# Moving the later adaLN modulation of a two-layer RWKV/mLSTM/retention trunk from DVE sums in the projection stage to column products on PE in the RWKV stage

## The chip, the cores and the metric

The kernel runs on one core of one Trainium2 chip. The core has a matrix engine (PE, with its weight loader PEld), three engines for elementwise work (DVE, ACT, POOL) and SP, whose queue issues every DMA of this kernel, one after the other. The metric is the device time of one execution in microseconds, as the median of several runs: 3966.14 us before, from three runs between 3945.2 and 3976.5.

## The reference, cut to what matters

The reference is one inference step of a two-layer trunk over 128 context tokens and 1024 noisy tokens, width 1024. Each layer modulates its normalised input and its output by a conditioning vector:

```python
mod = silu(c) @ w_mod[l] + b_mod[l]              # 1024 -> 3072: shift, scale, gate
h = rmsnorm(x, norm_g) * (1 + scale) + shift
u = h @ w_in                                     # one projection for four head groups
y = concat(mlstm(u_a), rglru(u_b), retention(u_c), rwkv(u_d)) @ w_out
x = x + gate * y
```

There are two conditioning vectors (context and sample), so a modulation is a product of a 1024 x 3072 matrix with two columns, once for each layer. It is small in arithmetic and large in weights: 12 MB for each layer.

## The kernel before, in words

All is float32, with tokens along the free dimension and 128 channels along the partitions. The modulation of a layer is cut into six blocks (l, j) of 512 outputs; a block reads eight weight tiles of 128 x 512 (256 KB each). Blocks (0, 0) to (0, 3), which give shift and scale of layer 0, are computed at the very start. The other eight, listed in `MODS`, are the later ones: (0, 4) and (0, 5) give the gate of layer 0, (1, 0) to (1, 5) all of layer 1.

A layer has two long stages.

**The projection stage** (`in_proj`) walks over a list of jobs. A job loads a tile of `w_in`, splits it into two halves `wring_h` and `wring_l` (ACT, POOL), and multiplies both with the halves `hh` and `hl` of the input on PE, 24 products for each output tile, into one of two PSUM tiles named `main`. DVE and ACT in turn copy the result out (`st`, L1306 and L1304), and a DMA stores it. The jobs of kind C have the weights stationary (`main<-hh,wring_h` in the rows), those of kind T the tokens (`main<-wring_h,hh`). The mLSTM, RG-LRU and retention branches run beside the jobs as soon as their inputs are there. In layer 0 alone, every fourth job starts one later modulation: for each of the eight weight tiles (`wmod`, two buffers) and each of the two columns, DVE multiplies the 128 x 512 tile by one number for each partition and adds it to `macc` (L52, L48). After three more jobs PE sums `macc` over the partitions by products with a column of ones (`main<-ones,macc`, eight products) in a `main` tile, and DVE adds the bias into `mod`.

**The RWKV stage** (`rw_all`) runs through nine units, in nine periods. In a period, a chain of 16 steps alternates between PE and DVE (`u<-ST,AR`, DVE `UV`; `u<-UV,BT`, DVE `ST`), and between two steps lies a gap. DVE meanwhile solves triangular blocks of the next unit (`tm`, `iN`), whose input and result pass through DRAM (`dU`, `dN`, `SC`). To keep PE at work in the gaps, `pull` takes products of two other projections: the projections of RWKV's own inputs (`late_proj`, weights `w_in`) and the output projection (`out_proj`, weights `w_out`). These products (`main<-yt,ow`, L1312), 648 in a layer, are called fills here. A fill's weights come in tiles of the tag `ow`, with six buffers (`OWB`), four fills to a tile.

In this stage the products on PE stand in the order of the program (`pe` chains each one to the one before it), so PE cannot pass a product that waits. Elsewhere, and on the other engines and SP, a scheduler sets the order when the kernel is built, by priorities (`level`, `HP1`, `HP2`) and by its own estimate of times. A float32 product of the program is two instructions on PE in the trace, each with its own weight load.

Of the kernel before, what the change touches and what calls it, by code (L numbers as in the profile page):

```python
# [30 lines left out]
class B:  # L31
# [130 lines left out]
    def rw_all(self, l):  # L162
# [83 lines left out]
        for n, (p, su) in enumerate(units):  # L246
# [6 lines left out]
            for gap in range(16):  # L253
                with self.level(3):
                    next(steps)
                self.pull(rate)
                if gap == 1 and finish is not None:
                    with self.level(1):
                        self.rw_gate(finish)
                        self.rw_final(l, finish)  # L260
                    self.finished += 1
                    finish = None
                if gap == 1 and n + 1 == N:
                    with self.level(1):
                        self.rw_gate(P[p])
                if gap >= 2:
                    next(tok, None)
                if gap == 4 and n + 2 < N:
                    block(n + 2)
                    pre = early(n + 2)  # L270
                if gap in (12, 14):
                    next(pre, None)
            weave(tok, 0)
            weave(pre, 0)
# [22 lines left out]
    def pull(self, x):  # L297

        self.credit += x
        while self.credit >= 1:  # L300
            self.credit -= 1
            next(self.fills, None)

    def drain(self, what):
# [803 lines left out]

    def modulation(self, l, j, pool):


        acc = [pool.tile([128, 512], F32, tag="macc%d" % e, name="macc") for e in range(2)]
        for k in range(8):
            w = pool.tile([128, 512], F32, tag="wmod", name="wmod", bufs=2)
            self.dma(w, self.i["w_mod"][l, j][:, k])
            for e in range(2):
                if k == 0:
                    self.ts(self.v, acc[e], w, self.sc[:, k, e:e + 1], MUL)
                else:
                    self.stt(self.v, acc[e], w, self.sc[:, k, e:e + 1], acc[e], MUL, ADD)  # L1120
        yield
        ps = self.pmain()[:, 0:8].rearrange("p (i c) -> p i c", c=2)
        for i in range(4):
            for e in range(2):
                self.mm(ps[:, i, e:e + 1], acc[e][:, 128 * i:128 * i + 128], self.ones[:, 0:1])
        self.tt(self.v, self.mod[l][:, 4 * j:4 * j + 4], ps,
                self.par["bmod"][:, 24 * l + 4 * j:24 * l + 4 * j + 4, None].broadcast_to([128, 4, 2]), ADD)

# [131 lines left out]

    def in_proj(self, l, wp, sp, mp, hh, hl):
        n = 0
        mods = [self.modulation(z, j, mp) for z, j in MODS] if l == 0 else []
        rh = wp.tile([128, 3, KT, 128], F32R, name="wring_h")
        rl = wp.tile([128, 3, KT, 128], F32R, name="wring_l")
        pos = 0
        for t_, (kind, name, p, tiles) in enumerate(JOBS):
            if name[:3] == "rw_" and p in LATE:
                continue
            if mods and t_ % 4 == 0:  # L1270
                next(mods[0])
            if mods and t_ % 4 == 3:
                next(mods.pop(0), None)
            nt = len(tiles)
# [100 lines left out]
    def build(self):  # L1375
# [10 lines left out]
        for l in range(2):  # L1386
# [7 lines left out]
            with self.ph as ph:  # L1394
                P = lambda n, b=1, **kw: ph.enter_context(tc.tile_pool(name=n + "_%d" % l, bufs=b, **kw, **tw))
                wp, sp = P("w"), P("st")
                self.in_proj(l, wp, sp, P("md") if l == 0 else None, *self.h)
                with tc.high_priority(offset=HP1), ExitStack() as st:
# [25 lines left out]
            with ExitStack() as ph:  # L1424
# [18 lines left out]
                self.fills, self.done, self.credit, self.pulled, self.finished = work(), set(), 0.0, 0, 0  # L1443
                self.nfill = 648
                self.rw_all(l)
            self.tail(l, (3,), lambda: self.open_h(1))
# [13 lines left out]
OWB, SO = 6, 3  # L1460
MODS = ((0, 4), (0, 5), (1, 0), (1, 1), (1, 2), (1, 3), (1, 4), (1, 5))
T12 = 2
# [163 lines left out]
```

## Time and profile before

| what | before |
|---|---|
| median of three runs | 3966.14 us |
| the profiled execution | 3965.97 us |
| its span | 3964.1 us |
| mean granted clock of TensorE | 0.923 of 2.4 GHz |
| PE, DVE, ACT, POOL busy | 91%, 53%, 33%, 28% |
| layer 0: projections until 1105 us, then the ends of the branches, RWKV until about 1960 us |  |
| layer 1: projections from 2037 to 3015 us, RWKV until about 3880 us |  |

The shares of busy time are averages over stages with different limits, so the stages are read apart. A row of a stretch gives its length and then, for each engine, busy time and number of instructions. PE's busy time counts overlapping instructions once, and PE's idle time in a stretch is its length less the busy time. The first stages of layer 0 and layer 1 do the same work on the same shapes, but for the later modulations, which are in layer 0 alone.

### The profile page before, as it was taken

Reading aid. Unit: us, or ns where it says so; the run is one execution under the profiler, and the core shown is the slowest. Engines: PE = TensorE matmul, PEld = TensorE weight load, DVE = VectorE, ACT = ScalarE, POOL = GpSimd, SP = SyncE. Lnnn points to the kernel's source line nnn. Section 1 sums busy time; section 2 is a strip of 40 time slices with the busy share of each in tenths; the row PEclk is TensorE's granted clock in tenths of the full one; section 3 lists DMA queues with packets and bytes.
Section 4 is the critical chain, followed back from the end, with each engine's and each line's share of the span. In section 5 each row is a group of like instructions: output and inputs, shape, how many; then the busy total and the mean of one; then the engine's idle time right before and its main releaser. Section 6 shows DMA issues by size and latency. Waiting matters only on the chain. (4 is left out here: it accounts for less than half of the span.)

```text
span 3964.1 us, 69608 instructions
## 1 busy us (share of the span) xinstructions
PE 3624.5 (91%) x28018; PEld 2850.2 (72%) x28018; DVE 2110.8 (53%) x4081; ACT 1290.7 (33%) x2094; POOL 1119.5 (28%) x1016
## 2 busy tenths in 40 slices
PE   5898999999978999899888999999998889988997
PEld 2897888999955656555568898999996555555554
DVE  6555656433336576667264545443423556776644
ACT  3233342212222343343142344322222234343313
POOL 4222323453331122211033232344243312122200
PEclk7898898999979999899989899999897999999999
DMA  6545354434335454434663343434333444434446
GB/s 229 147 119 138 114 151 135 136 122 136 121 99 156 132 162 112 116 120 127 186 210 112 105 136 122 127 119 144 109 122 127 131 148 137 134 104 121 125 138 201
DMA packets 413549, 538.00 MB, mean 136 GB/s; under 512 B 141708, under 2 KB 322700, under 8 KB 413228
## 3 DMA queue, kind: packets, MB, share of 16 engines
q1 hardware_dynamic: 413228, 533.57, 44.7%
q8 instruction: 220, 3.60, 0.4%
q14 instruction: 101, 0.83, 0.1%
HBM read 387.17 MB, written 146.25 MB: 135 GB/s over the span
## 5 line engine op out<-in xcount | busy, mean ns | idle before, releaser
L1312 PE MATMUL main<-yt,ow 128*128 128x384 f32 x2592 | 990.5, 520 | 21.3 <-DVE xi L48 17.4
L1312 PEld LDWEIGHTS main<-yt,ow 128*128 128x128 f32 x2592 | 476.0, 197 | 316.6 <-issue 45.5
L59 PE MATMUL main<-hh,wring_h 128*128 128x384 f32 x1824 | 654.7, 359 | 22.8 <-ACT hh L56 9.8
L59 PE MATMUL main<-hl,wring_h 128*128 128x384 f32 x1824 | 648.1, 355 | 20.2 <-DVE hl L44 17.6
L59 PE MATMUL main<-hh,wring_l 128*128 128x384 f32 x1824 | 647.7, 355 | 0.0
L44 POOL TENSOR_TENSOR wring_l<-raw,wring_h 128x1024 fp32r<-128x1024 f32 x100 | 249.9, 2504 | 571.2 <-ACT wring_h L1258 428.9
L59 PEld LDWEIGHTS main<-hh,wring_h 128*128 128x128 f32 x1824 | 363.1, 199 | 38.5 <-ACT hh L56 10.3
L59 PEld LDWEIGHTS main<-hl,wring_h 128*128 128x128 f32 x1824 | 362.9, 199 | 33.6 <-DVE hl L44 21.5
L59 PEld LDWEIGHTS main<-hh,wring_l 128*128 128x128 f32 x1824 | 362.6, 199 | 8.2 <-issue 2.0
L59 PE MATMUL main<-wring_h,hh 128*128 128x256 f32 x864 | 265.0, 307 | 25.7 <-DVE st L1306 25.0
L59 PE MATMUL main<-wring_l,hh 128*128 128x256 f32 x864 | 261.0, 302 | 0.0
L59 PE MATMUL main<-wring_h,hl 128*128 128x256 f32 x864 | 259.2, 300 | 0.0
L44 DVE TENSOR_TENSOR iN<-iN,tm 64x31 f32<-64x31 f32 (+15 forms) x558 | 201.5, 361 | 15.4
L44 DVE TENSOR_TENSOR tm<-iU,iN 64x31 f32<-64x31 f32 (+15 forms) x558 | 201.1, 360 | 15.1
L1306 DVE COPY st<-main 128x384 f32<-128x384 f32 (+1 forms) x168 | 85.8, 511 | 219.8 <-PE main L59 178.4
L59 PEld LDWEIGHTS main<-wring_h,hh 128*128 128x128 f32 x864 | 178.0, 206 | 32.0 <-DVE st L1306 26.1
L44 POOL TENSOR_TENSOR t<-s_k,bb 128x512 f32<-128x512 f32 x36 | 63.3, 1758 | 465.7 <-ACT bb L56 465.7
L59 PEld LDWEIGHTS main<-wring_h,hl 128*128 128x128 f32 x864 | 177.6, 206 | 4.0 <-issue 1.1
L59 PEld LDWEIGHTS main<-wring_l,hh 128*128 128x128 f32 x864 | 177.7, 206 | 2.7
L1258 ACT CAST wring_h<-raw 128x1024 fp32r<-128x1024 f32 x100 | 103.4, 1045 | 199.7 <-PE main L59 174.4
L1304 ACT COPY st<-main 128x384 f32<-128x384 f32 (+1 forms) x168 | 73.6, 438 | 270.6 <-PE main L59 259.9
L56 ACT ACT_TABLE_LOAD x123 | 157.8, 1283 | 3.0 <-PEq L1618 0.7
(331 smaller groups left out, 6104.0 us busy)
## 6 DMA issues: line engine op xcount, KB each, us to landing
raw<-in_w_in SPq DMA_DIRECT2D x100, 512.0 KB, 4.1
ow<-in_w_in SPq DMA_DIRECT2D x144, 256.0 KB, 3.6
ow<-in_w_out SPq DMA_DIRECT2D x144, 256.0 KB, 2.7
yt<-h SPq DMA_DIRECT2D x144, 192.0 KB, 4.5
mrb<-mlrow SPq DMA_DIRECT2D x48, 384.0 KB, 4.1
x<-xi SPq DMA_DIRECT2D x96, 192.0 KB, 2.9
yt<-y SPq DMA_DIRECT2D x90, 192.0 KB, 3.2
wmod<-in_w_mod SPq DMA_DIRECT2D x64, 256.0 KB, 3.7
```

Of the source, the lines that this page charges most:

```text
L44: return e.tensor_tensor(out=out, in0=a, in1=b, op=op)
L56: return self.a.activation(out=out, in_=a, func=f, scale=scale, bias=bias)
L59: return self.t.matmul(out, l, r, start=start, stop=stop)
L1258: self.a.copy(hi, raw)
L1304: self.a.copy(q[:, :w], ps[:, :w])
L1306: self.v.tensor_copy(q[:, :w], ps[:, :w])
L1312: return self.pe(self.t.matmul(*a, **k))
```

## The change

`modulation` no longer uses DVE or `macc`. It takes two blocks at a time, and for each weight tile it issues four products on PE with a 128 x 128 piece of the tile as the stationary side and the two columns of silu(c) as the moving side. All 64 products of a pair of blocks add up in one PSUM tile of the tag `v`; two DVE additions of the bias end the pair. The weight tiles are taken from the six buffers of the fills (`tag="ow"`).

The generator now runs in the RWKV stage of layer 0, in the periods 1, 3, 6 and 7 of `MODS`: from the gap after step 4 on, `pull` takes two of its products after each fill, and the end of the loop of gaps takes what is left. `in_proj` has no modulation any more.

```diff
+                if gap == 4 and l == 0 and n in MODS:
+                    self.beside = self.modulation(MODS[n], self.wp)
+            for _ in self.beside:
+                pass
             weave(tok, 0)
...
             next(self.fills, None)
+            next(self.beside, None)
...
-    def modulation(self, l, j, pool):
-
-
-        acc = [pool.tile([128, 512], F32, tag="macc%d" % e, name="macc") for e in range(2)]
+    def modulation(self, blocks, pool):
+
+
+        ps = self.pst2("v")[:, :, 0:8].rearrange("p b (i c) -> p b i c", c=2)
         for k in range(8):
-            w = pool.tile([128, 512], F32, tag="wmod", name="wmod", bufs=2)
-            self.dma(w, self.i["w_mod"][l, j][:, k])
-            for e in range(2):
-                if k == 0:
-                    self.ts(self.v, acc[e], w, self.sc[:, k, e:e + 1], MUL)
-                else:
-                    self.stt(self.v, acc[e], w, self.sc[:, k, e:e + 1], acc[e], MUL, ADD)
-        yield
-        ps = self.pmain()[:, 0:8].rearrange("p (i c) -> p i c", c=2)
-        for i in range(4):
-            for e in range(2):
-                self.mm(ps[:, i, e:e + 1], acc[e][:, 128 * i:128 * i + 128], self.ones[:, 0:1])
-        self.tt(self.v, self.mod[l][:, 4 * j:4 * j + 4], ps,
-                self.par["bmod"][:, 24 * l + 4 * j:24 * l + 4 * j + 4, None].broadcast_to([128, 4, 2]), ADD)
+            for z, (l, j) in enumerate(blocks):
+                w = pool.tile([128, 1, 512], F32, tag="ow", name="wmod")
+                self.dma(w, self.i["w_mod"][l, j][:, k:k + 1])
+                for i in range(4):
+
+                    self.pm(ps[:, z, i], w[:, 0, 128 * i:128 * i + 128], self.sc[:, k], start=(k + i == 0), stop=(4 * k + i == 31))
+                    if i % 2:
+                        yield
+        for z, (l, j) in enumerate(blocks):
+            self.tt(self.v, self.mod[l][:, 4 * j:4 * j + 4], ps[:, z],
+                    self.par["bmod"][:, 24 * l + 4 * j:24 * l + 4 * j + 4, None].broadcast_to([128, 4, 2]), ADD)
...
-            if mods and t_ % 4 == 0:
-                next(mods[0])
-            if mods and t_ % 4 == 3:
-                next(mods.pop(0), None)
...
-MODS = ((0, 4), (0, 5), (1, 0), (1, 1), (1, 2), (1, 3), (1, 4), (1, 5))
+MODS = {1: ((0, 4), (0, 5)), 3: ((1, 0), (1, 1)), 6: ((1, 2), (1, 3)), 7: ((1, 4), (1, 5))}
```

**DVE in the projection stage of layer 0.** This is where one modulation ends and the next begins, beside the RG-LRU branch (`lr_`) and the mLSTM's norm (`ng`). Before:

```order
L48 SCALAR_TENSOR_TENSOR lr_h<-lr_h,lr_tr 128x1152
L52 TENSOR_SCALAR macc<-wmod,silu_c 128x512
L44 TENSOR_TENSOR mod_75<-main,p_bmod 128x8
L52 TENSOR_SCALAR macc<-wmod,silu_c 128x512
L48 SCALAR_TENSOR_TENSOR macc<-wmod,silu_c,macc 128x512 x2
L48 SCALAR_TENSOR_TENSOR lr_xc<-lr_xb,c_lr_cw,lr_xc 128x127
```

And now, at one of the same places:

```order
L48 SCALAR_TENSOR_TENSOR lr_h<-lr_h,lr_tr 128x1152
L1303 COPY st<-main 128x384
L44 TENSOR_TENSOR mkw<-mkt,ml_cols 128x3x128 x2
L44 TENSOR_TENSOR mhd<-mN,mdn 128x384
L1303 COPY st<-main 128x384
L48 SCALAR_TENSOR_TENSOR lr_xc<-lr_xb,c_lr_cw,lr_xc 128x127
```

The `macc` rows are gone from DVE, and the copies out of PSUM (`st`) stand nearer to each other. Without them, DVE's order in this stage is nearly the one that layer 1 had before.

**PE in the RWKV stage, period 1, gaps 6 and 7.** Rows of `main<-yt,ow` are fills, those of `u` are steps of the chain. Before:

```order
L59 MATMUL u<-UV,BT 64x64 x4
L1312 MATMUL main<-yt,ow 128x384 x3
L59 MATMUL a<-UV,SC 64x64 x16
L59 MATMUL u<-ST,AR 64x64 x4
L1312 MATMUL main<-yt,ow 128x384 x2
L62 MATMUL a<-ident,BK 128x128 x4
L59 MATMUL u<-UV,BT 64x64 x4
```

And now:

```order
L59 MATMUL a<-UV,SC 64x64 x16
L59 MATMUL u<-ST,AR 64x64 x4
L1309 MATMUL main<-yt,ow 128x384
L59 MATMUL v<-silu_c,wmod 128x2 x2
L1309 MATMUL main<-yt,ow 128x384
L59 MATMUL v<-silu_c,wmod 128x2 x2
L62 MATMUL a<-ident,BK 128x128 x4
L59 MATMUL u<-UV,BT 64x64 x4
```

Two products of the modulation stand behind each fill, between one step of the chain and the next.

**SP in the RWKV stage, period 6, around the result of the solve.** `dN` and `SC` carry the solve's result through DRAM; the first `dN` waits for DVE. Before:

```order
L81 DMA yt_15146<-y_2_3_0_8493 128x384
L81 DMA ow_15450<-in_w_out 128x512
L81 DMA dN_14674<-iN_14684 32x1024
L81 DMA out_rwkv_s<-ST_14795 128x64
L81 DMA out_rwkv_s<-ST_14796 128x64
L81 DMA dN_14674<-iU_14683 32x1024
L81 DMA SC_14545<-dN_14674 32x8x32 x4
L81 DMA SC_14648<-dN_14674 32x8x32 x4
L81 DMA x_0_0_7_12343<-xi_15039 128x384
L81 DMA ow_15452<-in_w_out 128x512
```

And now:

```order
L81 DMA wmod_14955<-in_w_mod 128x512
L81 DMA x_0_0_6_12096<-xi_14789 128x384
L81 DMA out_rwkv_s<-ST_14637 128x64
L81 DMA out_rwkv_s<-ST_14638 128x64
L81 DMA dN_14516<-iN_14526 32x1024
L81 DMA wmod_14963<-in_w_mod 128x512
L81 DMA dN_14516<-iU_14525 32x1024
L81 DMA yt_15063<-y_1_0_0_6910 128x384
L81 DMA SC_14387<-dN_14516 32x8x32 x4
L81 DMA SC_14490<-dN_14516 32x8x32 x4
L81 DMA wmod_14999<-in_w_mod 128x512
L81 DMA wmod_15013<-in_w_mod 128x512
```

Weight tiles that the same period's products need now stand between and behind the DMAs of the solve; before, the tile there was one that the fills needed later.

## Rows read from the trace of the kernel before

**Rows 1.** Stretches: length, busy us (x) PE, PEld, DVE, ACT, POOL; PEclk, DMA, GB/s.
```profile
140.30:1104.80 964.50, 926.96 (x5456) 868.45 (x5456) 473.77 (x697) 282.53 (x409) 340.90 (x318) 0.92 0.45 132
2103.60:3014.60 911.00, 885.81 (x5320) 832.43 (x5320) 391.17 (x576) 282.12 (x408) 322.96 (x318) 0.94 0.42 124
```

**Rows 2.** Timeline of PE: each stretch's first product of a T job.
```profile
140.34 0.58 PE L59 MATMUL main<-wring_h,hh 128*128 128x256 f32 x1 [10.53 <-DVE st L1306]
...
2103.65 0.58 PE L59 MATMUL main<-wring_h,hh 128*128 128x256 f32 x1 [8.41 <-DVE st L1306]
```

**Rows 3.** Groups on PE, layer 0's stretch: busy us, mean ns | idle before.
```profile
L59 PE MATMUL main<-hh,wring_h 128*128 128x384 f32 x840 | 303.9, 362 | 2.0 <-DVE st L1306 1.6 <-ACT st L1304 0.4
...
L59 PE MATMUL main<-ones,macc 128*128 128x1 f32 x112 | 16.0, 268 | 1.4 <-ACT st L1304 1.4
```

**Rows 4.** The same group in layer 1's stretch.
```profile
L59 PE MATMUL main<-hh,wring_h 128*128 128x384 f32 x840 | 296.7, 353 | 4.9 <-DVE st L1306 4.1 <-ACT st L1304 0.8
```

**Rows 5.** The instructions on `wmod`: duration ns min/median/max, first and last start.
```profile
L48 DVE SCALAR_TENSOR_TENSOR macc<-wmod,silu_c,macc x112: 730/746/2866, 39.7 to 765.9; 128x512 f32<-128x512 f32 x112
...
L52 DVE TENSOR_SCALAR macc<-wmod,silu_c x16: 470/481/2601, 37.0 to 749.7; 128x512 f32<-128x512 f32 x16
```

**Rows 6.** Waits of SP's queue, 100 to 860 us: us, times, longest.
```profile
SPq L81 <- DVE macc L48: 49.8, 33, 5.5
```

**Rows 7.** Timeline of DVE during the first norm: start us, us.
```profile
54.08 1.41 DVE L48 SCALAR_TENSOR_TENSOR macc<-wmod,silu_c,macc 128x512 f32<-128x512 f32 x2 [2.37 <-DMA wmod<-in_w_mod]
...
92.96 2.15 DVE L48 SCALAR_TENSOR_TENSOR macc<-wmod,silu_c,macc 128x512 f32<-128x512 f32 x2
```

**Rows 8.** Timeline of PE around products of one column.
```profile
442.25 2.56 PE L59 MATMUL main<-ones,macc 128*128 128x1 f32 x12
444.67 0.67 PE L59 MATMUL main<-hh,wring_h 128*128 128x384 f32 x1
...
745.08 0.50 PE L59 MATMUL main<-ones,macc 128*128 128x1 f32 x4
745.51 0.93 PE L59 MATMUL rS<-rtq,rtk 64*128 64x128 f32 x6
...
833.01 0.50 PE L59 MATMUL main<-ones,macc 128*128 128x1 f32 x4
833.38 0.52 PE L954 MATMUL rkt<-ident,rtk 128*128 128x128 f32 x3
```

**Rows 9.** Timeline of PE in period 3: one gap and the next step.
```profile
1540.63 0.34 PE L59 MATMUL u<-ST,AR 64*64 64x64 f32 x8
1540.90 2.20 PE L1312 MATMUL main<-yt,ow 128*128 128x384 f32 x6
1543.03 1.15 PE L59 MATMUL a<-UV,SC 64*64 64x64 f32 x32
1544.11 0.45 PE L59 MATMUL u<-UV,BT 128*64 128x64 f32 x8
```

**Rows 10.** Stretches: the periods 1, 3, 6 and 7 of layer 0.
```profile
1341.90:1414.60 72.70, 71.11 (x868) 45.55 (x865) 47.65 (x119) 24.24 (x47) 17.29 (x13) 0.95 0.48 137
1496.80:1567.00 70.20, 69.17 (x854) 44.21 (x854) 44.72 (x121) 22.62 (x44) 14.01 (x11) 0.98 0.43 120
1745.60:1821.70 76.10, 71.45 (x814) 44.92 (x814) 49.55 (x117) 29.86 (x59) 19.27 (x15) 0.97 0.44 128
1821.70:1892.60 70.90, 68.76 (x858) 44.31 (x858) 45.13 (x117) 21.07 (x36) 10.27 (x8) 0.98 0.40 117
```

**Rows 11.** Waits of PE in periods 6 and 7.
```profile
PE v L59 <- DMA SC<-dN: 3.4, 3, 2.0
```

**Rows 12.** The tiles `ow`: issue to landing.
```profile
DMA to landing us min/median/max: 2.6/3.2/6.1
```

**Rows 13.** Stretches of 20 us: clock in either stage.
```profile
440.00:460.00 20.00, 19.19 (x84) 17.28 (x85) 15.66 (x33) 6.07 (x9) 3.26 (x3) 0.77 0.67 197
...
1410.00:1430.00 20.00, 20.00 (x505) 14.66 (x504) 10.99 (x16) 6.08 (x17) 11.84 (x10) 1.00 0.30 84
```

More of the change, by code (lines that the diff above doesn't have):

```diff
@@ L1259, in split_w, with in_proj @@
         self.tt(self.g, lo, raw, hi.bitcast(F32), SUB)
-    def in_proj(self, l, wp, sp, mp, hh, hl):
+    def in_proj(self, l, wp, sp, hh, hl):
         n = 0
-        mods = [self.modulation(z, j, mp) for z, j in MODS] if l == 0 else []
         rh = wp.tile([128, 3, KT, 128], F32R, name="wring_h")
@@ L1396, in build @@
                 wp, sp = P("w"), P("st")
-                self.in_proj(l, wp, sp, P("md") if l == 0 else None, *self.h)
+                self.in_proj(l, wp, sp, *self.h)
                 with tc.high_priority(offset=HP1), ExitStack() as st:
@@ L1444, in build @@
                 self.nfill = 648
+                self.beside, self.wp = iter(()), wp
                 self.rw_all(l)
```

## The prediction, made before the changed kernel was run

> **What bounds the kernel now.** I first read the two projection stages as stretches, each from the first product of a T job [rows 2] to the stage's last product with `hh`. PE is busy for 926.96 of 964.5 us in layer 0 and for 885.81 of 911.0 us in layer 1 [rows 1], so PE bounds both. They do the same jobs; layer 0 alone has the later modulations, and its stretch is 53.5 us longer. That is the nearest thing to a measurement of what the change removes. Next I read the periods of the RWKV stage into which the new products go. PE is busy for 71.11 of 72.7, 69.17 of 70.2, 71.45 of 76.1 and 68.76 of 70.9 us [rows 10]: PE bounds these periods too, and what is added to it there has almost no idle time to go into. DVE, at 44.7 to 49.6 us in each period, is not the bound. So the change moves work between two stages that both hang on PE, and the result is a difference of two sums of nearly one size.
>
> **What it removes.** On DVE, 112 additions of 746 ns and 16 products of 481 ns, 91 us in all [rows 5]. DVE is busy for 474 of 964 us in that stretch [rows 1], so these 91 us don't count by themselves; they count where PE waits for a copy behind them. Three things are in the rows. PE has 37.5 us idle in layer 0's stretch and 25.2 us in layer 1's (length less busy), 12.3 us more. The products with ones take PE 16.0 us [rows 3]. The main products are slower, 362 ns against 353 ns [rows 3, 4], where the granted clock is 0.92 against 0.94 [rows 1]: the group shown has 840 instructions and is one of three of its length, so 2,520 by 9 ns are 23 us of durations; neighbours overlap in PE's pipeline, and I count half, about 10 us. SP waits 49.8 us for `macc` to let its two buffers go [rows 6], with stores and loads of the branches queued behind; that is inside the 53.5 us, as later starts. The parts that I can name make 38 us; the rest is the branches' products under the lower clock and what the rows don't split. I take the whole difference, **53 us**, since the new order of DVE, ACT and POOL in this stage of layer 0 is nearly layer 1's; 38 is the low end, and 60 the high one.
>
> Before that stretch, the first modulation's sums stand in DVE's way while the norm is on the path and PE waits for it: 1.4 and 2.2 us at the two places shown [rows 7], and a few like them. With the products with ones ahead of the stretch and less traffic at the start I take **6 us**, from 3 to 9.
>
> **What it adds on PE.** Eight blocks of 32 products are 256 products, or 512 instructions, each a 128 x 128 weight load with two columns streamed. The trace has no such product, but the products of one column over the same weight shape are as near as can be. Four of them between other products take 0.43 us from start to next start at 745.08 and 0.37 us at 833.01, so 0.100 us each; at half clock, twelve take 2.42 us, 0.202 us each [rows 8]. The low end is the row of small steps, eight 64 x 64 instructions in 0.27 us, 0.034 us each [rows 9]: 17 us. The high end is 103 us. I take 0.100, as the new groups of four stand between other products just so: **51 us**. The fill before hides the first load of a group, and the fill behind has its own load exposed, which the groups of four also contain.
>
> The Trainium skill ("TensorE: Matmul & The Clock Gate", section "Back-to-back issue gap") gives about 81 ns for each pair of weight load and small product in a sustained stream; the sum would then be, as an estimate, 41 us and the total 10 us less. The rows here say 0.092 to 0.107 us, and the measurement decides.
>
> **What it adds in waits.** The 64 weight tiles take turns in the fills' six buffers. Before, a buffer came round every 24 fills; now two modulation tiles pass for every four fills beside the one tile of the fills, so it comes round every eight. A gap takes 3.48 us for three fills [rows 9], 1.16 us for each; with 0.40 us of new products it is 1.56, and eight fills are 12.5 us. A fill's tile is held for four fills, so on average about 6 us are left for its successor, against a landing of 3.2 us in the median and 6.1 us at most [rows 12]. On average it is enough, but in periods 6 and 7 a projection takes three tiles at once and holds the last one for twelve fills, and some tiles can only be asked for two or three fills before their product. PE's order is fixed, so it stands still until the tile lands, and with it the chain. SP is one queue: behind a tile that waits for a buffer, and behind `dN`, which waits for the end of the solve, all later DMAs wait too. For 90 tiles in four periods (64, and about 26 of the fills) nothing is the low end and 1 us each the high one; I take about ten that come 1 us late, **10 us**.
>
> **What covers it.** PE's wait for the solve's result in periods 6 and 7, 3.4 us [rows 11], goes if the period is longer: **-4 us** with small ones. If DVE falls behind in the now fuller gaps, the same wait comes back. The bias additions are eight on DVE, with some 4 us of PE's products between the last product and the next use of `v`: nothing. The DMAs are 64 before and 64 after. For the clock I take **4 us**.
>
> **The sum** is made against the profiled 3965.97 us, which is the median (3966.14) within 0.2 us: 3966 - 53 - 6 + 51 + 10 - 4 + 4 = **3968 us**, no change that a measurement of this kernel can tell; its three runs before span 0.8%, so 1%, 40 us, is what counts as a change. This case's own range is 3940 to 3998.
>
> **The rivals.**
> 1. **The buffers run dry** (slower). In the four periods nearly every tile is late: the landing of 3.2 us, and SP blocked behind `dN` or a store, eats the 6 us that are left. It decides from the point at which a tile is asked for less than about 4 us before its product. One us for each of the 64 tiles instead of ten of them is 3968 + 54 = **4022 us**. For it speaks that SP's queue is in order and that the tiles stand around `dN`; against it, that fills before had room of 24.
> 2. **The products hide** (faster). PE's weight loads run ahead under the fills' streams, PEld being busy only 44 to 46 us of each period [rows 10], and the products cost half, 25 us; the first stage gives 60 and its start 6, and nothing waits: 3966 - 66 + 25 - 4 = **3921 us**. Against it: the groups in the rows have the same chance to hide, and take 0.100 us each.
> 3. **The clock falls in the gaps.** With sparse products the clock was 0.77 in the one stretch of the first stage and 1.00 in the RWKV stage at 505 small instructions in 20 us [rows 13]. If the four periods, some 340 us with the new products, of which two thirds are in the gaps, went from 0.97 to 0.87, that is 230 x 0.115 = 26 us: **3990 us**. The trace speaks against it, since the RWKV stage keeps its clock with smaller instructions than these. The Trainium skill (the same page, section "A second HAM failure mode: psum-queue depth-cycling") says that short idle times between groups of products make the clock swing between its two levels; by that rule this would be what happens, and the row at 1.00 doesn't bear it out.
> 4. **The change doesn't do what it says**: the excess of layer 0 has another cause (its start from a cold pipeline), and only the products with ones and part of the idle time go, 25 us: 3968 + 28 + 6 = **4002 us**.
>
> **How the numbers follow.** The forecast has 0.62, the dry buffers 0.18, the hidden products 0.12, the clock 0.05, the other cause 0.03. Slower by over 1% (above 4006 us) is most of the second case and a tail of the others, 0.17; faster by over 1% (below 3926) is most of the third and a little of the first, 0.12; within 1% is 0.71. The range of 3920 to 4025 us takes in the forecast's own range and, on either side, the rivals' times.
>
> **What would show it.** In the changed profile, layer 0's stretch from the first T job to the last product should take 905 to 925 us and PE's idle time in it about 25; periods 1, 3, 6 and 7 should each be 13 to 17 us longer, the others as before; the products on `wmod` should come in groups of four 0.10 us apart; waits of PE for `wmod` or `ow` should sum to about 10 us. The prediction is wrong if those waits make 30 us or more, if the clock in the four periods falls below 0.92, or if the first stage stays above 940 us.

## The result, and the profile after

The changed kernel takes 3992.51 us in the median of ten runs, the kernel before 3959.68 us in ten runs on the same chips; the ratio is 1.0083, with a 95% interval of 1.0061 to 1.0106. So the change makes the kernel slower by 0.8%, 33 us: inside the 1% that the prediction counted as no change, inside its range of 3920 to 4025 us, and 25 us above its forecast of 3968 us. That forecast stood on a profiled run of 3966 us; as a change it was +2 us, and +33 us came. The profiled execution has a span of 3991.5 us against 3964.1 us, 27.4 us more, and the accounts below are made against these two spans.

The two projection stages of the changed kernel, each from the first product of a T job to the last product with `hh` (columns as in [rows 1]):

```profile
127.70:1036.20 908.50, 882.52 (x5345) 829.88 (x5344) 400.25 (x583) 284.23 (x411) 327.14 (x319) 0.95 0.41 125
...
2110.70:3034.20 923.50, 887.27 (x5345) 833.54 (x5343) 394.21 (x582) 284.46 (x411) 330.59 (x319) 0.94 0.42 123
```

Layer 0's stage takes 908.5 us where it took 964.5 [rows 1]: 56 us less. It also begins 12.6 us earlier (127.7 against 140.3), so its end comes 68.7 us earlier.

Here a row of mine has to be put right. The second row of [rows 2], at 2103.65, is not the first product of a T job in layer 1; it stands behind the wait in the middle of that job. The first one is at 2092.21, and the stretch of before is then:

```profile
2092.20:3014.70 922.50, 888.95 (x5345) 835.27 (x5344) 402.39 (x583) 284.93 (x411) 327.25 (x319) 0.94 0.42 123
```

The two layers of the kernel before thus differed by 42 us and not by 53.5, and PE's idle time in layer 1 was 33.6 us and not 25.2. A border has to be the same event in both stretches, found as the first of its kind.

The periods 1, 3, 6 and 7 of the changed kernel, now each from the first `v<-ident,SC` to the next one:

```profile
1273.30:1359.10 85.80, 83.03 (x990) 59.93 (x988) 49.76 (x123) 25.62 (x51) 17.86 (x14) 0.98 0.56 165
1438.30:1536.00 97.70, 88.38 (x990) 62.50 (x988) 50.75 (x127) 24.28 (x48) 17.43 (x14) 0.93 0.45 133
1711.90:1807.50 95.60, 93.13 (x946) 66.57 (x942) 52.75 (x123) 30.50 (x63) 22.52 (x20) 0.88 0.51 152
1807.50:1904.40 96.90, 92.01 (x994) 67.51 (x993) 44.68 (x117) 21.66 (x37) 7.67 (x5) 0.88 0.44 126
sum 376.00, PE 356.56 PEld 256.50 DVE 197.94 ACT 102.06 POOL 65.49; mean PE 89.14 PEld 64.13 DVE 49.48 ACT 25.52 POOL 16.37
```

By the same borders the kernel before has 72.7, 73.3, 77.8 and 74.0 us, 297.8 in all (those of [rows 10] were drawn a few us later). The four periods have grown by 78.2 us. The growth is uneven, 13 us in period 1, as forecast, and 18 to 24 us in the others, where the forecast had 13 to 17, though each has the same 64 products; and where it is large, the clock stands at 0.93 or 0.88, where it was 0.96 to 0.98.

PE's waits from period 0 to period 8, as us in all, times, longest:

```profile
PE v L59 <- DMA wmod<-in_w_mod: 9.9, 4, 3.9
...
PE v L59 <- DMA SC<-dN: 2.5, 2, 2.2
```

PE waits four times for a late weight tile, once in each period (1.2, 3.9, 2.5 and 2.4 us). The wait for the solve's result, 10.0 us from period 0 to 8 before, and 3.4 in the stretches of [rows 11], has shrunk to 2.5. Now PE around the wait in period 6 (columns: start, us, instruction, idle time before it and what ended it):

```profile
1779.26 0.91 PE L1309 MATMUL main<-yt,ow 128*128 128x384 f32 x2
1780.01 0.50 PE L59 MATMUL v<-silu_c,wmod 128*128 128x2 f32 x4
1780.38 0.89 PE L1309 MATMUL main<-yt,ow 128*128 128x384 f32 x2
1783.73 1.02 PE L59 MATMUL v<-silu_c,wmod 128*128 128x2 f32 x4 [2.47 <-DMA wmod<-in_w_mod]
1784.68 0.49 PE L59 MATMUL u<-ST,AR 64*64 64x64 f32 x8
1785.11 1.65 PE L1309 MATMUL main<-yt,ow 128*128 128x384 f32 x2
1786.55 0.85 PE L59 MATMUL v<-silu_c,wmod 128*128 128x2 f32 x4
```

Ahead of the wait, four instructions of the modulation take 0.37 us from start to next start, 0.09 us each, and the two of a fill 0.75 us. Behind it everything takes twice as long: 0.71 us and 1.44 us. SP in the same microseconds shows why the tile was late:

```profile
1773.32 0.38 SPq L81 DMA_DIRECT2D dN<-iN  x1
1773.79 0.38 SPq L81 DMA_DIRECT2D wmod<-in_w_mod  x1
1774.26 0.39 SPq L81 DMA_DIRECT2D dN<-iU  x1
1774.70 0.41 SPq L81 DMA_DIRECT2D yt<-y  x1
1775.37 5.20 SPq L81 DMA_DIRECT2D SC<-dN  x8
1780.66 1.34 SPq L81 DMA_DIRECT2D wmod<-in_w_mod  x3
```

The tile's DMA is asked for at 1780.66, behind eight transfers `SC` that occupy SP's queue for 5.2 us, and lands just before 1783.73. All four late tiles stand behind such a group of `SC`, in period 7 with five other DMAs between. The clock ahead of, behind and after two of the waits, as stretches:

```profile
1770.00:1783.70 13.70, 11.27 (x77) 7.63 (x75) 5.18 (x18) 4.15 (x6) 0.60 (x1) 1.00 0.63 170
1783.70:1807.60 23.90, 23.87 (x168) 17.98 (x172) 8.48 (x17) 3.25 (x9) 10.20 (x10) 0.50 0.55 175
1807.60:1820.00 12.40, 12.40 (x324) 8.46 (x325) 3.28 (x6) 3.52 (x9) 0.36 (x1) 1.00 0.21 50
...
1879.30:1903.20 23.90, 23.90 (x166) 19.14 (x165) 1.29 (x6) 0.00 (x0) 0.00 (x0) 0.50 0.31 95
```

The granted clock is 1.00 (2.4 GHz) up to the wait, 0.50 (1.2 GHz) for 23.9 us behind it, though PE is busy for all of them, and 1.00 again when the period's products of the modulation are over (the last one stands at 1801.3 us in period 6). A wait of 2.5 us thus costs about 2.5 + 12 us. Behind period 3's wait the half clock lasted 10.2 us, behind that of period 1 (1.2 us) there was none.

My theory from this: the products cost what was forecast; what was not forecast is the half clock, which four waits for tiles stuck behind `SC` set off. The rivals: the sparse products lower the clock by themselves, or the six buffers come round too fast, whichever queue asks.

### The profile page after: what moved, and what is told of

The parts are those of the page before. It is cut to its first block, busy times and chain, and to the rows that moved or that the text cites. A ratio compares the mean times of both kernels' runs of the same rounds, so it can differ in the third digit from the quotient of the medians.

```text
span 3991.5 us, 70203 instructions
## 1 busy us (share of the span) xinstructions
PE 3659.0 (92%) x28402; PEld 2889.6 (72%) x28402; DVE 2010.9 (50%) x3953; ACT 1290.2 (32%) x2094; POOL 1101.7 (28%) x1016
## 5 line engine op out<-in xcount | busy, mean ns | idle before, releaser
L1309 PE MATMUL main<-yt,ow 128*128 128x384 f32 x2592 | 1022.9, 528 | 24.8 <-DVE xi L48 20.2
L59 PE MATMUL main<-hh,wring_h 128*128 128x384 f32 x1824 | 645.8, 354 | 27.0 <-DVE st L1303 13.5
L59 PE MATMUL main<-wring_h,hh 128*128 128x256 f32 x864 | 262.3, 304 | 17.6 <-DVE st L1303 17.1
L59 PE MATMUL main<-wring_l,hh 128*128 128x256 f32 x864 | 258.0, 299 | 0.0
```

Source lines behind the costliest of these rows:

```text
L59: return self.t.matmul(out, l, r, start=start, stop=stop)
L1309: return self.pe(self.t.matmul(*a, **k))
```

## The experiments

Twelve further runs were made, eleven of new kernels and one of the change again. `e1_none`, `e2_one_tile`, `e10_few_after` and `e12_few_in_7` leave work out, to price it. Ratios are to the kernel before on the same chip, with 95% intervals.

| run | ratio | interval | median us | periods 1, 3, 6, 7: sum us |
|---|---|---|---|---|
| the change | 1.0083 | 1.0061 to 1.0106 | 3992.5 | 376.0 |
| e1_none | 0.9826 | 0.9806 to 0.9845 | 3894.9 | 297.8 |
| e2_one_tile | 0.9981 | 0.9965 to 0.9996 | 3955.2 | 340.7 |
| e3_act_queue | 1.0004 | 0.9986 to 1.0021 | 3963.2 | 345.8 |
| e4_spread | 1.0022 | 0.9999 to 1.0044 | 3968.9 | eight periods |
| e5_four | 1.0032 | 1.0005 to 1.0059 | 3969.8 | 352.8 |
| e6_act_pool | 1.0079 | 1.0055 to 1.0102 | 3991.9 | eight periods |
| e7_in_proj | 1.0140 | 1.0119 to 1.0161 | 4017.7 | none |
| e8_period8 | 1.0041 | 1.0021 to 1.0061 | 3972.9 | period 8 for 7 |
| e9_in_act_pool | 1.0072 | 1.0050 to 1.0094 | 3984.0 | none |
| e10_few_after | 1.0051 | 1.0018 to 1.0084 | 3983.1 | 366.8 |
| e11_again | 1.0086 | 1.0063 to 1.0108 | 3990.4 | 377.9 |
| e12_few_in_7 | 1.0010 | 0.9974 to 1.0045 | 3969.0 | 358.4 |

**e1_none: the removal alone.**

```diff
...
-                    self.pm(ps[:, z, i], w[:, 0, 128 * i:128 * i + 128], self.sc[:, k], start=(k + i == 0), stop=(4 * k + i == 31))
...
+            self.v.tensor_copy(self.mod[l][:, 4 * j:4 * j + 4],
+                               self.par["bmod"][:, 24 * l + 4 * j:24 * l + 4 * j + 4, None].broadcast_to([128, 4, 2]))
```

> Left out: the eight later modulations (weights, products); only their bias is copied, in the same four periods. This prices the removal alone, and by its difference to the change the cost of the products with all that hangs on them. Theory: periods 1, 3, 6, 7 fall back to about 73, 73, 78 and 74 us, so 78 us under the change's 3992: 3914 us, and the first stage of layer 0 ends near 1036 us as in the change. Second theory, that the 20 us by which the second layer was longer in the change's profile are chance and not its order: 3895 us. Rival, that the gain of the first stage is given back elsewhere whatever stands in the RWKV stage: above 3930 us.

Measured: 3894.9 us, the second theory's number. Periods 6 and 7 of this kernel:

```profile
1677.10:1755.40 78.30, 71.95 (x811) 45.03 (x811) 49.01 (x117) 29.03 (x56) 17.95 (x14) 0.96 0.43 123
1755.40:1831.20 75.80, 70.35 (x862) 45.40 (x862) 47.87 (x119) 21.92 (x40) 13.01 (x9) 0.95 0.42 113
```

The four periods sum to 297.8 us, just as before, so all of their growth comes from the products and what hangs on them. Taking the later modulation out of the first stage is worth 1.7%, 69 us; the end of that stage moved by 68.7 us in the change. The gain is not given back elsewhere.

**e2_one_tile: the products without their transfers.**

```diff
-                w = pool.tile([128, 1, 512], F32, tag="ow", name="wmod")
-                self.dma(w, self.i["w_mod"][l, j][:, k:k + 1])
+                if k + z == 0:
+                    w = pool.tile([128, 1, 512], F32, tag="wmod", name="wmod", bufs=1)
+                    self.dma(w, self.i["w_mod"][l, j][:, k:k + 1])
```

> Left out: 60 of the 64 weight tiles; all products of a pair of blocks read one resident tile, so every product stays and nearly no weight transfer does. Theory (late tiles, and the low clock that follows a stall): the products alone cost 46 us over the kernel without modulation, no wait for a weight tile, clock 0.95 or more in periods 3, 6 and 7, time about 3960 us. Rival (the sparse products pull the clock down by themselves): clock in periods 6 and 7 stays at 0.88 to 0.90 and the time at 3980 us or more.

Measured: 3955.2 us. Periods 6 and 7:

```profile
1698.80:1783.00 84.20, 82.36 (x944) 59.05 (x945) 53.04 (x123) 30.81 (x63) 18.54 (x16) 1.00 0.46 129
1783.00:1866.40 83.40, 80.53 (x992) 58.98 (x990) 45.27 (x118) 21.67 (x37) 12.28 (x9) 1.00 0.35 96
```

All 512 instructions are there, no tile is late, and the clock is 1.00 in both (0.98 in periods 1 and 3). So the sparse products do not lower the clock by themselves in these periods: the rival falls. Their price is the difference to e1_none in the four periods: 340.7 - 297.8 = 42.9 us, which is 47.7 us more of busy PE (328.9 against 281.2) less 4.8 us of idle time that they fill. The clock flatters this price: these four periods hold 6.8 us at half clock, those of e1_none 20.4, which is worth up to 7 us.

**e3_act_queue: another queue for the weight tiles.**

```diff
-                self.dma(w, self.i["w_mod"][l, j][:, k:k + 1])
+                self.a.dma_start(out=w, in_=self.i["w_mod"][l, j][:, k:k + 1])
```

> All weight tiles of the later modulation are asked for by ACT's queue, not SP's, from the same six buffers. Theory (on SP a tile stands behind the eight transfers SC of the solve): the four waits for wmod, 10 us, and the half clock behind them go, periods 3, 6 and 7 take 86 to 90 us each, time about 3962 us. Rival (the six buffers come round too fast, whichever queue asks): waits for wmod stay near 10 us, time about 3990 us. Third case: ACT itself stands still for a buffer and its copies come late; then PE waits for ACT appear in the gaps, time above 3990 us.

Measured: 3963.2 us. Periods 6 and 7:

```profile
1705.90:1794.70 88.80, 84.33 (x942) 59.97 (x938) 53.94 (x123) 30.64 (x63) 20.66 (x18) 0.98 0.56 167
1794.70:1878.20 83.50, 80.77 (x994) 58.94 (x990) 44.69 (x117) 21.67 (x37) 9.92 (x7) 1.00 0.51 147
```

PE's wait for the tiles from period 0 to 8:

```profile
PE v L59 <- DMA wmod<-in_w_mod: 1.5, 3, 0.9
```

The same six buffers, the same 64 transfers, and the waits fall from 9.9 to 1.5 us, the clock goes up, and by the ratios 31 of the 33 us are back. So the buffers are enough, and SP's order was the trouble. The waits of PE for ACT did not grow. One wait of 2.4 us remains in period 6, for a fill's tile `ow`, and no half clock follows it.

**e4_spread: one block in each of eight periods.**

```diff
-MODS = {1: ((0, 4), (0, 5)), 3: ((1, 0), (1, 1)), 6: ((1, 2), (1, 3)), 7: ((1, 4), (1, 5))}
+MODS = {n: (z,) for n, z in enumerate(((0, 4), (0, 5), (1, 0), (1, 1), (1, 2), (1, 3), (1, 4), (1, 5)))}
```

> One block in each of the periods 0 to 7 instead of two in each of four. The products behind one fill stay two, so they end after 16 fills and no weight tile but the first period's stands behind the transfers SC. Theory (the stall behind SC is what is dear): each of the eight periods grows by about 6 us, waits for wmod at most 3 us, no long half clock, time about 3962 us. Rival (buffers run dry by the rate of two products behind each fill): waits for wmod near 10 us, time about 3990 us.

Measured: 3968.9 us; waits for `wmod` 0.3 us, as the theory has it, but one long half clock all the same. Period 4, and the stretch of half clock in it:

```profile
1540.00:1654.10 114.10, 101.38 (x973) 67.43 (x969) 63.47 (x162) 39.24 (x81) 25.13 (x27) 0.82 0.34 95
1580.70:1608.00 27.30, 26.52 (x127) 19.23 (x126) 14.55 (x37) 5.02 (x9) 1.26 (x1) 0.50 0.39 116
```

One of PE's waits from period 0 to 8:

```profile
PE v L59 <- DVE bs L44: 8.3, 7, 2.8
```

In periods 0 and 4 a new pair's sums (`bs`) use the same PSUM tag `v` in which a modulation adds up, and PE waits for DVE. Period 4 grew from 92.2 to 114.1 us; its half clock sets in at a wait of 2.0 us for DVE, not for a tile. How much of that is the tag and how much the clock was not taken apart.

**e5_four: four of the 64 tiles.**

```diff
+FOUR = ((0, 4, 5), (1, 1, 4), (1, 2, 6), (1, 5, 5))
-                self.dma(w, self.i["w_mod"][l, j][:, k:k + 1])
+                (self.a if (l, j, k) in FOUR else self.s).dma_start(out=w, in_=self.i["w_mod"][l, j][:, k:k + 1])
```

> The change, with four of its 64 weight tiles asked for by ACT's queue: just the four for which PE waited in the change's profile (1.2, 3.9, 2.5 and 2.4 us), all of which stood behind the transfers SC on SP. Theory (these four waits and the half clock behind them are what the change lost over its products): periods 3, 6 and 7 fall to 86 to 90 us, no half clock of 24 us, time 3960 to 3968 us. Rival (the rate at which the buffers come round is the cause, and the next tile will be late instead): waits for wmod stay at 8 us or more, the clock in periods 6 and 7 below 0.92, time 3980 us or more.

Measured: 3969.8 us. PE's waits from period 0 to 8:

```profile
PE main L1309 <- DMA ow<-in_w_out: 1.6, 1, 1.6
PE v L59 <- DMA wmod<-in_w_mod: 1.4, 3, 0.7
```

Its period 6:

```profile
1696.50:1788.40 91.90, 88.67 (x942) 63.62 (x939) 53.93 (x123) 30.60 (x63) 22.70 (x20) 0.93 0.53 161
```

Four transfers moved, and by the ratios 20 us are back; the time is 1.8 us above the theory's range. Period 6 keeps a half clock of 10 us, behind a fill's tile that comes 1.6 us late. No other tile of the modulation was late in their place: the rival falls.

**e6_act_pool: the sums on ACT and POOL in the RWKV stage.**

```diff
...
+                    self.act(q, w[:, 0], ACT.Copy, scale=self.sc[:, k, e:e + 1])
+                    self.tt(self.g, acc[e], acc[e], q, ADD)
...
```

> The sums go to engines that are idle in the RWKV stage: ACT multiplies a weight tile by one number for each partition, POOL adds it to macc, one block in each of the periods 0 to 7; on PE stay eight products with ones for a block, at its period's end. The fills' input buffers are 14, not 16, to make room. Theory (PE is the bound, so what leaves PE is saved): 3895 us of the kernel without modulation and 128 instructions at 0.1 us, some waits of a chain step for ACT: 3905 to 3925 us. Rival (POOL's additions, 1.4 us each, and ACT's, 0.63 us, come between the solve's and the tokens' own work, and PE waits for POOL or ACT): 3950 us or more.

Measured: 3991.9 us; the rival was right, by another engine than it named. From period 0 to 8:

```profile
1196.80:1931.40 734.60, 629.10 (x6983) 396.08 (x6985) 505.99 (x1030) 330.49 (x576) 287.98 (x214) 0.91 0.45 134
```

PE's longest wait there:

```profile
PE u L59 <- DVE UV L44: 34.4, 15, 7.5
```

The same stretch of e1_none:

```profile
1194.50:1831.20 636.70, 584.03 (x6851) 366.48 (x6850) 427.97 (x1026) 244.29 (x448) 131.98 (x102) 0.96 0.44 129
```

DVE has four instructions more and is busy for 78 us longer, 506 against 428, beside a POOL that is busy for 288 us instead of 132. ACT is busier too, 330 us against 244, but DVE's instructions that met ACT alone took as long as those that met neither; those that met POOL took 1.3 to 2.0 times as long. An idle engine was not a free one: the chain's DVE steps came late.

**e7_in_proj: the column products in the first projection stage.**

```diff
+            ws = [pool.tile([128, 512], F32, tag="wmod", name="wmod", bufs=4) for k in range(4)]
...
+                    self.mm(ps[:, i], ws[k][:, 128 * i:128 * i + 128], self.sc[:, 4 * h + k], start=(k + i == 0), stop=(k + i == 6))
```

> The column products on PE, but in the first projection stage, where the sums were: four weight tiles at a time, 16 products in one group, two groups for a block, into a tile main; nothing in the RWKV stage. Theory (the gain of the change is the sums that leave DVE, its cost the products, wherever they stand): 3895 us and the products' 512 instructions at 0.09 to 0.1 us: 3940 to 3950 us. Rival (the groups take one of the two tiles main and idle the main products, or lower the clock there): the stage ends later than 1100 us, time 3960 us or more.

Measured: 4017.7 us. The stage, and a stretch in it, with the 13.7 us ahead of that:

```profile
143.40:1162.90 1019.50, 984.46 (x5792) 924.16 (x5792) 381.66 (x585) 280.71 (x408) 319.58 (x318) 0.90 0.43 125
226.20:239.90 13.70, 13.70 (x87) 12.71 (x86) 8.21 (x13) 3.64 (x5) 4.12 (x4) 1.00 0.58 175
239.90:246.70 6.80, 6.77 (x22) 5.62 (x22) 5.46 (x12) 2.10 (x3) 2.15 (x3) 0.50 0.40 105
```

Most of a group of 32 on PE, where the clock falls:

```profile
237.73 3.56 PE L59 MATMUL main<-silu_c,wmod 128*128 128x2 f32 x26
```

The stage is 111 us longer than in the change, with PE busy for all but 35 us of it, and it holds 199 us at half clock against 92. The clock fell to half in the midst of a group of sparse products, with no idle time of PE ahead of it. That is not peculiar to these groups: behind a row of the mLSTM's products of 65 columns (`mN`) it falls without idle time as well, here at 502.7 us, for 23.9 us, in which 32 instructions of the modulation stand, and in the change's first stage at 258.0 us, for 6.8 us. So the rival on the clock, wrong for the RWKV periods, is right here. In the RWKV stage the products cost 43 us by themselves and 78 with what hangs on them; here it is 111.

**e8_period8: the last pair in period 8, on ACT's queue.**

To the edit of e3_act_queue comes this:

```diff
-MODS = {1: ((0, 4), (0, 5)), 3: ((1, 0), (1, 1)), 6: ((1, 2), (1, 3)), 7: ((1, 4), (1, 5))}
+MODS = {1: ((0, 4), (0, 5)), 3: ((1, 0), (1, 1)), 6: ((1, 2), (1, 3)), 8: ((1, 4), (1, 5))}
```

> As the run with ACT's queue, and the last pair of blocks stands in period 8 in place of period 7; nothing before the second layer's output reads it. Theory (in the kernels with products in period 7 DVE's order at the second layer's norm and PE's order behind it came out worse, 6 to 10 us from period 8 to the first T job and 8 to 15 us in the second projection stage against the kernel without modulation): period 7 falls to 75 us, period 8 takes some 10 us more, the second projection stage takes 905 to 915 us, time 3945 us. Rival (that part of the second layer differs from kernel to kernel with no regard to where the products stand, or comes with any products): 3960 us or more.

Measured: 3972.9 us; my theory fell. Period 7, and from period 8 to the first T job:

```profile
1795.90:1867.40 71.50, 67.17 (x864) 43.60 (x862) 43.91 (x115) 21.66 (x37) 7.78 (x5) 1.00 0.39 108
1867.40:2096.20 228.80, 190.87 (x1262) 138.65 (x1259) 101.67 (x220) 64.17 (x107) 43.43 (x37) 0.90 0.58 190
```

Period 7 fell as expected, but the products cost 22.7 us in period 8 and behind it (206.1 in e3_act_queue), and the second projection stage took 926 us, as in e3_act_queue (927).

**e9_in_act_pool: the old place, ACT and POOL for DVE.**

```diff
...
-                    self.stt(self.v, acc[e], w, self.sc[:, k, e:e + 1], acc[e], MUL, ADD)
...
+                    self.act(q, w, ACT.Copy, scale=self.sc[:, k, e:e + 1])
+                    self.tt(self.g, acc[e], acc[e], q, ADD)
```

> The kernel before, its sums in the first projection stage as they were, but ACT multiplies by the number for each partition and POOL adds; DVE has none of it. Theory (what cost there was DVE's 91 us and its copies, which came late; ACT and POOL are busy for a third of that stage): the stage falls most of the way to the change's 908 us, time 3910 to 3930 us with the products with ones left. Rival (POOL's additions come between its halves of the weights, and ACT's between the weights' and the copies out, and PE waits for these; DVE slows down beside POOL): the stage stays above 960 us, time 3950 us or more.

Measured: 3984.0 us, as the rival. The stage:

```profile
145.40:1116.80 971.40, 921.54 (x5456) 863.21 (x5456) 424.58 (x584) 353.80 (x517) 469.54 (x415) 0.92 0.46 131
```

PE's longest wait in it, and the same wait in the kernel before:

```profile
PE main L59 <- DVE st L1308: 29.0, 9, 10.5
...
PE main L59 <- DVE st L1306: 18.1, 7, 10.5
```

DVE is busy for 49 us less than in [rows 1], and the stage is 7 us longer, not shorter. This does not price DVE's 91 us: PE waited longer for DVE's copies, 29.0 us against 18.1, beside a POOL that is busy for 470 us instead of 341, so one cost took the place of another. What else stayed in the stage are the 112 products with ones, the clock of 0.92, and SP's waits for the sums (56.5 us, 49.8 in [rows 6]). Which of them the 69 us were is not shown.

**e10_few_after, e11_again, e12_few_in_7: why the half clock lasts.** In the two kernels with fewer products all transfers stay; `e10` leaves out 12 products behind period 6's wait (its first line reads `(l, j) in ((1, 2), (1, 3)) and k >= 6`), `e12` 15 behind that of period 7:

```diff
+                few = (l, j) in ((1, 4), (1, 5)) and 2 * k + j >= 15
-                    self.pm(ps[:, z, i], w[:, 0, 128 * i:128 * i + 128], self.sc[:, k], start=(k + i == 0), stop=(4 * k + i == 31))
+                    if i == 0 or not few:
+                        self.pm(ps[:, z, i], w[:, 0, 128 * i:128 * i + 128], self.sc[:, k], start=(k + i == 0), stop=(k == 7 and i == (0 if few else 3)))
```

> The change, with 12 of the last 16 products of period 6 left out: those of the last four weight tiles but one for each tile. They stand behind the wait for the late tile; all transfers stay, and SP's order is the same up to there, so the wait of 2.5 us stays. Period 7 is left as it was, and is the control in the same run. Theory (the sparse products behind the wait keep the clock at half): the half clock behind period 6's wait lasts 10 us or less, that of period 7 some 24 us again, period 6 takes 84 to 88 us. Rival (the wait alone sets it): half clock of some 24 us in both periods, period 6 at 92 to 95 us.

> The changed kernel once more, for a second trace. Theory (the four waits are fixed by the order on SP): PE waits for wmod at the same four tiles, 9 to 11 us in all, half clocks of some 24 us in periods 6 and 7, 3985 to 4000 us. Rival (waits and clock of the first trace were chance): waits at other tiles, or a clock above 0.95 in period 6 or 7.

> The change, with 15 of the last 20 products of period 7 left out: those of the last five weight tiles but one for each tile, all behind the wait for the tile that came late there in three of three traces of the same order (2.4, 3.2, 3.0 us, each followed by 23.9 us at half clock). Transfers and SP's order are the same up to that wait. Theory (the sparse products behind the wait keep the clock at half): wait of 2.4 us or more again, half clock behind it 3 to 10 us, period 7 at 80 to 86 us. Rival (the wait alone sets it): half clock of some 24 us again, period 7 at 90 us or more. The time of the whole kernel does not decide: 3975 to 3990 us by either.

The repeat, e11_again, took 3990.4 us. Half clock behind period 3's wait, and period 6, in its trace:

```profile
1512.30:1546.40 34.10, 34.10 (x176) 24.21 (x176) 9.80 (x20) 5.46 (x11) 8.17 (x7) 0.50 0.29 87
...
1725.90:1812.90 87.00, 84.06 (x942) 60.12 (x938) 53.41 (x123) 30.49 (x63) 21.36 (x20) 0.98 0.55 167
```

The waits came again, 9.3 us in the four periods, 3.4 us in period 3 and 3.0 us in period 7. In period 6 they were only 1.2 and 1.0 us this time, and no long half clock followed; in period 3 it lasted 34.1 us instead of 10.2. With a clock of 0.98 in period 6 the rival's mark is met there. So the waits come from the order, and how long the half clock behind them lasts varies from run to run. In e10_few_after period 6 fell to 84.4 us at a clock of 1.00, but its wait for the modulation was 1.5 us, so on its own question the run decides nothing. e12_few_in_7 has its wait, in PE's timeline:

```profile
1875.63 0.59 PE L59 MATMUL v<-silu_c,wmod 128*128 128x2 f32 x2 [3.00 <-DMA wmod<-in_w_mod]
```

The stretches behind it:

```profile
1874.70:1881.50 6.80, 5.87 (x19) 3.75 (x20) 0.58 (x2) 0.00 (x0) 0.00 (x0) 0.50 0.57 176
1881.50:1889.40 7.90, 7.90 (x153) 6.26 (x151) 0.71 (x4) 0.00 (x0) 0.00 (x0) 1.00 0.50 155
```

Behind a wait of 3.0 us the half clock lasts 6.8 us with a quarter of the products, against 23.9 us in each of the three traces with all of them (behind 2.4, 3.2 and 3.0 us). Period 7 takes 84.7 us, and the whole kernel 3969.0 us, less than the 3975 to 3990 that were expected. So in period 7 the products behind the wait prolong the half clock; this rests on one trace against three.

It is no rule for the other periods. In period 3 the clock was back after 10.2 us in three of four traces, with 37 to 40 instructions of the modulation still to come. In the change's trace (length, PE's busy time on `wmod` alone with the number of instructions, clock, DMA, GB/s):

```profile
1510.70:1520.90 10.20, 2.56 (x12) 0.50 0.29 91
1520.90:1533.00 12.10, 4.91 (x40) 1.00 0.52 156
```

Nor is every wait of this length enough. In e10_few_after PE waits as long for a fill's tile in period 6, among the few products of the modulation that are left there, and that period has no half clock at all:

```profile
1800.52 1.56 PE L1310 MATMUL main<-yt,ow 128*128 128x384 f32 x4 [2.45 <-DMA ow<-in_w_out]
```

In the change and these three runs, every half clock of more than 10.2 us in the four periods had a wait of PE for a weight tile at its start or 2 us ahead of it, and sparse products behind it (in period 6 of e12_few_in_7 1.7 us of waiting and 17.1 us of half clock). Neither was enough alone for a long one (e2_one_tile, e10_few_after), and what sets its length stays open.

## Why the prediction was right, and where it was not

Its range and its likeliest answer, no change beyond 1%, held; the sign inside that 1% is now known, and the forecast is 25 us short.

| term | forecast, us | measured, us | from |
|---|---|---|---|
| start and first stage | -59 | -68.7 | end of the stage |
| products on PE | +51 | +47.7 | e2_one_tile less e1_none, PE busy in the four periods |
| waits covered | -4 | -4.8 | the same, PE idle |
| late tiles | +10 | +9.9 | waits for `wmod` |
| clock | +4 | +25.4 | 376.0 less 340.7, less 9.9 |
| everything else | 0 | +18 | the two spans |

**The first stage.** 53 was taken from two stretches, one of them with a wrong border; rightly read they gave 42, and the stage gave 56. That the number lies near is luck. The parts that I named were 12.3 us of idle time, 16.0 us of products with ones and 10 us of slower products; by the right border the first of them, the difference of the two layers, was 3.9 us. Measured were 11.5 us less idle time (37.5 to 26.0) and 44.4 us less of busy PE, of which 16.0 us are the products with ones. The other 28.4 us came at a clock whose share I had put too low: the stage had 162 us at half clock before, and 92 after. The start gave 12.6 where 6 was forecast.

**The products.** Groups of four cost 0.091 us for each instruction in the median at full clock, where the rows gave 0.092 to 0.107. The rival in which they hide has no support: e2_one_tile, where nothing waits, still pays 42.9 us.

**The waits.** The sum was right, the picture not, so the sum is luck: four waits of 1.2 to 3.9 us, not ten of 1 us, and not by the buffers' rate but behind `SC`. The rule that some tiles would come late because "SP is one queue" was the right half of that paragraph. The rival of dry buffers, at 54 us more, did not occur.

**The clock** is the step that failed. I gave it 4 us, and a chance of 0.05 to a rival of 26 us, since "the RWKV stage keeps its clock with smaller instructions than these". That is true where no tile of the modulation is late by more than 0.9 us, as e2_one_tile and e3_act_queue show at 0.98 to 1.00. Measured are 25.4 us: the four periods of the change hold 64.9 us at half clock, those of e2_one_tile 6.8. So the time came out at that rival's 3990 us, but not by its mechanism, in which the products lower the clock with no wait. I did not put the two terms together: each late tile was priced at its wait, when a wait of 2.4 us or more came with half clock every time it occurred for `wmod` (nine times in the four traces that have the change's order around it: 6.8 to 34.1 us). Two waits of 2.4 us for a fill's tile, in e3_act_queue and e10_few_after, did not. The kernel before showed half the answer: its periods too have stretches of half clock behind idle times of PE, but these last 3.4 to 10.2 us. The prediction's own mark, a clock below 0.92 in the four periods, is met in periods 6 and 7 at 0.88 (0.91 over all four).

The Trainium skill ("TensorE: Matmul & The Clock Gate", section "HAM oscillation — how this bites in real kernels") tells of a kernel of thin products whose clock falls at each wait for a DMA. The traces agree where PE waited 2.4 us and more for `wmod`. That section tells of no fall without a wait; e7_in_proj fell to 0.50 at 239.9 us with no idle time in the 13.7 us before.

**Everything else**, 18 us, was forecast at nothing: 6.7 us from period 8 to the first T job of layer 1, where DVE does eight `xs<-xs,sg` in a row and PE waits 8.2 us for `hl`; 5.8 us in the periods of layer 1, which were gone in e11_again (631.5 us, 636.7 before); the rest in small pieces. The second projection stage took between 906 and 931 us over these kernels, though no instruction of it was edited. e8_period8 tested one cause, products in period 7, and it was not that. What sets it stays open.

None of the versions beats the kernel before. The best that computes everything, e3_act_queue, is level with it: the 69 us that the first stage gives are paid back by 43 us of products in a stage that PE bounds as well, and by some 20 us elsewhere.

## What to carry to other kernels

Price a late transfer in front of sparse products not at its wait but at the clock behind it: here, with all products in place, 2.4 to 3.9 us of waiting came with 10 to 34 us at half speed. When loads are added to a queue, look for the group of transfers in it that waits for something else, and at what stands right behind that group; four DMAs on another queue were worth 20 of 33 us. And before work is moved from one stage to another, ask what bounds the second: both hung on PE, so the move could at best win the difference of two prices.

## What the runs showed of the hardware that I had not expected

- DVE slowed down beside POOL: nearly the same instructions (four more) took 506 us instead of 428 when POOL was busy for 288 us instead of 132 (e6_act_pool against e1_none). Its `tm<-iU,iN` of 64 x 175 went from 330 to 706 ns in the mean, its `BK<-ta,t` of 128 x 256 from 776 to 884. Beside ACT alone its instructions kept their time.
- The clock fell to half with no idle time of PE ahead of it, where 32 small instructions stood in one group among wide products (e7_in_proj, 239.9 us), and behind rows of products of 65 columns (`mN`; e7_in_proj, 502.7 us, and the change, 258.0 us).
- The same small instruction, in groups of four between fills, left the clock at 1.00 where no tile was late (e2_one_tile, periods 6 and 7). Behind a wait in period 7 the half clock was shorter with fewer of them (6.8 us in e12_few_in_7, 23.9 in three traces); in period 3 the clock came back among them after 10.2 us.
